# Two decoder blocks in one kernel: attention by pairs of heads, another order on ScalarE around a triangular inversion, and four PSUM banks in turn

## The chip, the cores and the metric

One Trainium2 chip, of which one core is used. The metric is device time in microseconds (us) of one execution of the whole program, from the first to the last instruction and what lies around them; lower is better. TensorE (PE) multiplies, VectorE (DVE), ScalarE (ACT) and GpSimd (POOL) work element by element, SyncE (SP) issues most DMAs. All five take their instructions in the order of their own queue.

## What is computed

`x` holds 512 tokens of 1024 features in float32. Two different blocks follow one another, each with two layers.

```python
# block 1, per layer
h = rms_norm(x, norm_mix[l])
(m_qk, m_v, m_o, m_i, m_f, r_x, r_g, a_q, a_k, a_v, a_qi, a_ki, a_w, gates) = split(h @ w_in[l])
y_a = mLSTM(silu(conv(m_qk)), m_v, m_i, m_f) * sigmoid(m_o)        # 4 heads of 128
y_b = gelu(r_g) * rg_lru(conv(r_x), ...)
y_c = dsa_attention(rope(a_q), rope(a_k), a_v, rope(a_qi), rope(a_ki), a_w)   # 8 heads of 64
x = x + (sum of sigmoid(gate_b) * (y_b' @ w_branch[b]) over the 3 branches) @ w_out[l]
x = x + (gelu(conv(ff_g)) * ff_u) @ ffn_down[l]
# dsa_attention, for each block of 128 queries:
score = sum_h w[q,h] * relu(q_idx[q,h] . k_idx[s]);  keep the 128 best visible keys of each query
p = softmax over those keys of q.k / 8;  out = p @ v
# block 2, per layer: RWKV-7 (chunks of 64 tokens), pooling branch, gates, gated FFN
S_t = S_{t-1} (diag(w_t) - kk_t^T (a_t*kk_t)) + v_t k_t^T ;  y_t = S_t r_t
y = (group_norm(y) * lnx_g + lnx_b + sum(r*k*r_k) * v) * g
```

## The kernel before

All activations lie transposed, 128 features by 512 tokens to a tile. A dense product of 128 output features (`lin_steps`, L490) takes 8 tiles of input; weights and inputs are each split into a rounded part H and a rest L of type float32r, and three matmuls (wh·hH, wh·hL, wl·hH) make up one step of the sum. 24 matmuls of 512 columns are one such product; each takes a PSUM bank by a tag and leaves it to a function of evacuation. Weights come by DMA from SP into three `raw` buffers; ACT casts them to `wh` (L432), DVE or POOL subtract to get `wl` (L433).

The program is written with generators that yield: `together` takes one step of each in turn, so dense products stand between the small steps of attention, mLSTM or RWKV ("fill"). A planner then orders each engine's queue by this written order, a cost model and due times; what it puts into a queue is fixed before the run.

**Block 1, `mix1`.** After the products for values, indexer and rope come `keys` (products aq and ak, with `dsa_mask` beside them), then `together(dsa(...), fill, beside())`, where `beside` holds the products qk, mv and mo. `dsa_mask(j)` makes for each of 8 indexer heads a product of two matmuls (L818 with all 128 rows, L819 with the 64 rows of one half), and finds the best 128 keys in 16 rounds on DVE (L831, L832). It runs for j = 1, 2, 3, with 128(j+1) keys. `dsa_attend(j)` goes head by head: one plain float32 matmul over 64 rows for the logits (L845), a softmax on DVE and ACT, up to four transposes (L861), and j+1 plain float32 matmuls with 64 output columns for the values (L868). The profile has two records for each plain float32 matmul. Then `mlstm` computes its gates (L893 to L917) and its heads; `rglru` and three `merge`s follow. PSUM's eight banks are shared as lin 3, pv 1, pb 2, at 2.

**Block 2, `mix2`.** `Rwkv.prep` and `prep_r` make decayed keys and queries for four pairs of heads (ksq L1550, rnb L1561, ar L1593 and L1603) beside the products 2k and 2r. `invert` multiplies them (am L1642), copies blocks into `room` and inverts 32 x 32 triangles by a serial chain on DVE (L1654 to L1668), beside a fill of 31 steps (`lent(fill, 31)`: products 2v, 2p, 2g1). `ready(0)` copies the inverse back (L1682, in turn on ACT, DVE and POOL), transposes it (L1685) and starts the chain of the chunks with L1689 (px). The evacuation of product 2v calls `bonus` (L1606 to L1624); that of 2p is the ACT copy `yb` (L1386), after which `pool` works on DVE (L1393 to L1398).

Of the kernel before, what the change touches and what calls it, by code (L numbers as in the profile page):

```python
# [9 lines left out]
F32 = mybir.dt.float32  # L10
# [8 lines left out]
KD = 8  # L19
# [291 lines left out]
def kernel(ctx: ExitStack, tc: tile.TileContext, aps: dict, out: bass.AP, taps=None, stop=None,  # L311
# [33 lines left out]
    def MX(name, tag="lin"):  # L345
        return cur[tag][0].tile([128, 512], F32, name=name, tag="p" + tag)
# [127 lines left out]
    def lin_steps(key, mts, hs, evac, first=0, last=0, tag="lin", fine=0):  # L474
# [19 lines left out]
        if first:  # L494
            ps = [MX("lnt", t) for t in {"at": ("at", "at", "lin", "lin"), "T2": ("T2",) * 3,
                                         "x": ("x", "x", "x", "lin")}[first_of("at", "T2", "x")][:first]]
# [13 lines left out]
        for m in range(first, mts - last):  # L510
            units = {g: u for g, u in units.items() if g >= m // gm}
            fetch(m, None)
            ps = MX("lnt", tag if isinstance(tag, str) else tag[m % len(tag)])
# [18 lines left out]
    def lin_tokens(key, l, hs, evac):  # L532
# [3 lines left out]
        ps = [MX("lnt", t) for t in ("at", "at", "lin", "lin")]  # L536
# [181 lines left out]
    def merge(*a):  # L718
        for _ in merge_steps(*a):
            pass  # L720

    def merge_steps(key_g, key_b, l, hs, ys, merged, tag, ytag, fine=0, done=None):
# [22 lines left out]
        sg, sb = lin_steps((key_g, l), 8, hs, evg, fine=fine), lin_steps((key_b, l), 8, yhl, evb, fine=fine)  # L745
# [91 lines left out]
    def dsa_attend(j, q, k, v, mk, yc):  # L837
        wd = 128 * (j + 1)
# [19 lines left out]
        def transposed(h):  # L858
            tp = MX("tp", "at")
# [11 lines left out]
        for h in range(8 + 4):  # L871
            if h < 8:
                softmax(h)
                yield
            if 0 <= h - 2 < 8:
                transposed(h - 2)
                yield
            if h >= 4:
                values(h - 4)
                yield  # L880
# [9 lines left out]
    def mlstm(smt, l, q, k, v, mo, ya):  # L890
# [3 lines left out]
        T1 = U("T1", "t")  # L894
        G.memset(T1, 0.0)
        af = U("af", "t")
# [3 lines left out]
        ls = U("ls", "t")  # L900
        V.tensor_scalar(ls[r], smt[rf], ifb[rf], 0.0, op0=ALU.add, op1=ALU.min)
        V.tensor_sub(ls[r], ls[r], af[r])
        ip = U("ip", "t")
        V.tensor_scalar(ip[r], smt[r], ifb[r], None, op0=ALU.add)
        g = U("g", "t")
        V.tensor_tensor_scan(g[r], C("ones")[r, 0:1].to_broadcast([4, S]), ls[r], 0.0, op0=ALU.mult, op1=ALU.add)
        m = U("m", "t")
        V.tensor_tensor_scan(m[r], ls[r], ip[r], 0.0, op0=ALU.add, op1=ALU.max)
        gm = U("gm", "t")
        V.tensor_sub(gm[r], g[r], m[r])  # L910
# [609 lines left out]
    class Rwkv:  # L1520
# [14 lines left out]
        def prep(self, p):  # L1535
# [22 lines left out]
            for _ in range(3):  # L1558
                yield
# [341 lines left out]
```

## Time and profile before

| | |
|---|---|
| median of 3 runs | 3645.12 us (3644.09 to 3647.41) |
| profiled execution, its own time | 3652.54 us |
| its span, first to last instruction | 3650.1 us |
| PE busy | 3537.1 us, 97% |
| DVE, ACT, POOL busy | 59%, 41%, 21% |
| mean granted clock of PE | 0.986 of full speed |

A matmul's duration in the profile holds the way through the array, and the next one starts before it ends; what a matmul takes of PE's time is the distance from its start to the next start. A form such as 64*128 gives the rows and columns of the array that a matmul uses.

### The profile page before, as it was taken

What the parts mean: (1) busy time and instruction counts of PE and PEld (TensorE: products, weight loads), DVE (VectorE), ACT (ScalarE), POOL (GpSimd) and SP (SyncE); (2) the same over time, 40 slices, a digit from 0 to 9 for tenths busy, and PEclk for the clock granted to TensorE, in tenths of its full rate; (3) what the DMA queues carried; (4) which work ended last, traced back from release to release, by engine and by line L of the source; (5) the groups of instructions that cost most, each with busy time, mean ns of one, the idle gap of its engine ahead of it and who ended that gap; (6) DMA issues with size and microseconds to landing.
All of it is one profiled execution on the core that took longest, in us unless ns stands there. A gap on an engine that the chain in (4) does not pass through costs nothing.

```text
span 3650.1 us, 48877 instructions
## 1 busy us (share of the span) xinstructions
PE 3537.1 (97%) x18160; PEld 2806.6 (77%) x18160; DVE 2160.7 (59%) x4586; ACT 1503.1 (41%) x2838; POOL 776.8 (21%) x637
## 2 busy tenths in 40 slices
PE   7999999999999999999999988999999889999998
PEld 6667788888886677888888766788888757788887
DVE  6864535666658546356767785564345884473445
ACT  4555533333335546233333544333223544342223
POOL 3523311000035233110000463320000652320000
PEclk9999999999999999999999989999999989999999
DMA  4212232455522123224545211222223211322222
GB/s 134 90 49 68 94 98 93 145 180 167 173 77 89 49 68 101 92 99 136 186 153 176 83 64 56 90 93 93 93 96 108 75 56 58 102 93 87 98 93 75
DMA packets 124894, 367.61 MB, mean 101 GB/s; under 512 B 14704, under 2 KB 19056, under 8 KB 124656
## 3 DMA queue, kind: packets, MB, share of 16 engines
q1 hardware_dynamic: 119264, 357.15, 29.7%
q10 hardware_dynamic: 5392, 7.35, 0.8%
q8 instruction: 142, 2.33, 0.3%
q14 instruction: 96, 0.79, 0.1%
HBM read 350.28 MB, written 7.34 MB: 98 GB/s over the span
## 4 chain that ended last, share of the span: by engine, by line
PE 87%; DVE 9%; ACT 2%; issue 1%; DMA 1%; POOL 0%; SPq 0%; DVEq 0%; ACTq 0%; POOLq 0%
PE lnt L490 77%; PE at L845 1%; PE pv L868 1%; DVE tm L1662 1%; PE lnt L548 1%; DVE sums L1665 1%; DVE bk L1590 1%; PE am L1642 1%; DVE wl L433 1%; DVE hn L634 1%; PE tp L861 1%; PE sp L941 0%; PE is L819 0%; ACT wh L432 0%; DVE hL L644 0%
## 5 line engine op out<-in xcount | busy, mean ns | idle before, releaser
L432 ACT CAST wh<-raw 128x512 fp32r<-128x512 f32 x1096 | 669.5, 619 | 1503.5 <-PE lnt L490 1423.3
L490 PE MATMUL lnt<-hH,wh 128*128 128x512 f32 (+1 forms) x3184 | 1264.4, 398 | 20.6 <-ACT yb L1386 18.7
L490 PE MATMUL lnt<-hL,wh 128*128 128x512 f32 (+1 forms) x3184 | 1227.7, 386 | 2.1 <-DVE hL L644 2.1
L490 PE MATMUL lnt<-hH,wl 128*128 128x512 f32 (+1 forms) x3184 | 1229.2, 386 | 0.0
L433 DVE TENSOR_TENSOR wl<-raw,wh 128x512 fp32r<-128x512 f32 x772 | 538.6, 706 | 649.8 <-ACT wh L432 646.9
L433 POOL TENSOR_TENSOR wl<-raw,wh 128x512 fp32r<-128x512 f32 x324 | 440.2, 1364 | 1482.2 <-ACT wh L432 1438.7
L490 PEld LDWEIGHTS lnt<-hH,wh 128*128 128x128 f32 x3184 | 603.0, 190 | 190.7 <-issue 44.0
L490 PEld LDWEIGHTS lnt<-hL,wh 128*128 128x128 f32 x3184 | 604.0, 190 | 130.3 <-issue 9.8
L490 PEld LDWEIGHTS lnt<-hH,wl 128*128 128x128 f32 x3184 | 603.2, 189 | 130.4 <-issue 2.7
L490 PE MATMUL lnt<-fH,wh 128*128 128x512 f32 (+1 forms) x864 | 313.9, 364 | 0.0
L490 PE MATMUL lnt<-fL,wh 128*128 128x512 f32 (+1 forms) x864 | 313.3, 363 | 0.1
L490 PE MATMUL lnt<-fH,wl 128*128 128x512 f32 (+1 forms) x864 | 312.8, 362 | 0.0
L490 PEld LDWEIGHTS lnt<-fL,wh 128*128 128x128 f32 x864 | 163.0, 189 | 28.5 <-DVE fL L408 0.5
L490 PEld LDWEIGHTS lnt<-fH,wh 128*128 128x128 f32 x864 | 163.0, 189 | 28.3
L490 PEld LDWEIGHTS lnt<-fH,wl 128*128 128x128 f32 x864 | 163.0, 189 | 27.7
L590 POOL TENSOR_TENSOR sums<-sums,sq 128x256 f32<-128x256 f32 (+1 forms) x61 | 54.3, 896 | 562.9 <-ACT sq L588 561.8
L1301 DVE SCALAR_TENSOR_TENSOR x<-lnt,mod,x 128x512 f32<-128x512 f32 (+1 forms) x136 | 88.9, 655 | 88.3 <-PE lnt L490 88.0
L696 DVE SCALAR_TENSOR_TENSOR cv<-lnt,vec,cv 128x511 f32<-128x511 f32 (+1 forms) x168 | 124.1, 745 | 14.7 <-ACT cv L694 13.2
L490 PE MATMUL lnt<-yH,wh 128*128 128x512 f32 x320 | 129.3, 404 | 0.0
L490 PE MATMUL lnt<-yH,wl 128*128 128x512 f32 x320 | 127.7, 399 | 0.0
L490 PE MATMUL lnt<-yL,wh 128*128 128x512 f32 x320 | 126.8, 396 | 0.0
L1282 DVE CUSTOM_DVE_ANT_0 adaw<-adaw,csilu 128x512 f32<-128x512 f32 x192 | 125.0, 686 | 1.3 <-DMA adaw<-in_ada_dram 1.1
(393 smaller groups left out, 4280.1 us busy)
## 6 DMA issues: line engine op xcount, KB each, us to landing
raw<-in_wst_dram SPq DMA_DIRECT2D x548, 512.0 KB, 3.3
adaw<-in_ada_dram SPq DMA_DIRECT2D x192, 256.0 KB, 3.4
sw<-rq ACTq DMA_DIRECT2D x96, 64.0 KB, 2.0
xd<-x SPq DMA_DIRECT2D x16, 256.0 KB, 3.1
x<-xd SPq DMA_DIRECT2D x16, 256.0 KB, 3.5
x<-in_xT_dram SPq DMA_DIRECT2D x8, 256.0 KB, 6.0
out_dram<-x SPq DMA_DIRECT2D x8, 256.0 KB, 2.2
csilu<-in_c_dram SPq DMA_DIRECT2D x4, 256.0 KB, 5.4
```

The lines of the kernel that those rows point to most:

```text
L432: A.copy(h[:, :q], raw[:, sl])
L433: sub(l[:, :q], raw[:, sl], h[:, :q].bitcast(F32), op=ALU.subtract)
L490: mm = T.matmul(ps[:, sl], w_, h_[:, sl], start=(k == 0 and i == 0), stop=(k == kt - 1 and i == 2))
L548: T.matmul(ps[t], h_[:, o], w_, start=(k == 0 and i == 0), stop=(k == KD - 1 and i == 2))
L590: G.tensor_tensor(acc[:, sl], acc[:, sl], sq[:, sl], op=ALU.add)
L634: V.scalar_tensor_tensor(h, x[k][:, sl], g[:, k:k + 1], sums[0][:, sl], op0=ALU.mult, op1=ALU.mult)
L696: V.scalar_tensor_tensor(y[:, d:], ps[:, :S - d], taps_w[nt - 1 - d], y[:, d:], op0=ALU.mult, op1=ALU.add)
L845: T.matmul(ps[:, :wd], q[p][r, j * 128:j * 128 + 128], k[p][r, :wd], start=True, stop=True)
L861: T.transpose(tp[:, i * 128:i * 128 + 128], lgs[h][:, i * 128:i * 128 + 128], ident)
L868: T.matmul(pv[r, p * 128:p * 128 + 128], v[i][:, h * 64:h * 64 + 64], pts[h][:, i * 128:i * 128 + 128], start=(i == 0), stop=(i == j))
L1282: V.tensor_tensor_reduce(out=w, in0=w, in1=t, scale=1.0, scalar=0.0, op0=ALU.mult, op1=ALU.add, accum_out=sm[:, i:i + 1])
L1301: return V.scalar_tensor_tensor(x[m][:, sl], ps[:, sl], md[:, o + m:o + m + 1], x[m][:, sl], op0=ALU.mult, op1=ALU.add)
```

## The change

**Block 1.** q and k leave rope as H and L parts (one ACT copy and one DVE subtraction per tile, 8 tiles a layer). `logits(p)` makes the logits of two heads with six float32r matmuls, three terms, the two heads in turn, each into its own bank of a two-bank tile. `values(p)` runs the two heads of a pair in turn. L819 now takes all 128 rows. The mLSTM gates (`mgates`) run beside the attention of the last block of queries; six steps of dense work come ahead of the attention. The convolved qk tiles are kept in `x`, which is fetched again before the merges (from the input in layer 0, from a copy in DRAM in layer 1). Banks are now lin 2, pv 1, pb 3, and one tile of two banks, a2; the products of keys and of the merges take banks of several tags in turn.

**Block 2.** The copy rnb waits until ksq of the next pair is in ACT's queue. `bonus` is cut in two: `values` stays in the evacuation of 2v, the rest comes 14 matmul groups later, as one DVE multiplication from PSUM; the bias is added in `gate`. The first four of the fill's 31 steps come ahead of `invert`. The copies of `ready(0)` are all on DVE.

```diff
-    def MX(name, tag="lin"):
-        return cur[tag][0].tile([128, 512], F32, name=name, tag="p" + tag)
+    def MX(name, tag="lin", banks=1):
+        return cur[tag][0].tile([128, banks * 512], F32, name=name, tag="p" + tag)
...
             A.copy(q, ps)
-            lst.append(U(nm, tag))
-            rope(q, 128, lst[m], ps)
+            o = U("ro", "t")
+            rope(q, 128, o, ps)
+            lst.append(split(o, nm, tag))
...
-            qe, high = qi[p][e], slice(64 * e, 64 * e + 64)
-            T.matmul(ps[:, :wd], qe[:, j * 128:j * 128 + 128], kid[0][:, :wd], start=True, stop=False)
-            T.matmul(ps[:, :wd], qe[high, j * 128:j * 128 + 128], kid[1][high, :wd], start=False, stop=True)
+            qe = qi[p][e]
+            for i, t in enumerate(kid):
+                T.matmul(ps[:, :wd], qe[:, j * 128:j * 128 + 128], t[:, :wd], start=(i == 0), stop=(i == 1))
...
-        def softmax(h):
-            p, r = h // 2, slice(64 * (h % 2), 64 * (h % 2) + 64)
-            ps = MX("at", "at")
-            T.matmul(ps[:, :wd], q[p][r, j * 128:j * 128 + 128], k[p][r, :wd], start=True, stop=True)
+        def logits(p):
+            (qh, ql), (kh, kl) = q[p], k[p]
+            at = MX("at", "a2", 2)
+            pss = [at[:, e * 512:e * 512 + 512] for e in range(2)]
+            for i, (q_, k_) in enumerate(((qh, kh), (ql, kh), (qh, kl))):
+                for e, ps in enumerate(pss):
+                    r = slice(64 * e, 64 * e + 64)
+                    T.matmul(ps[:, :wd], q_[r, j * 128:j * 128 + 128], k_[r, :wd], start=(i == 0), stop=(i == 2))
+            return pss
+
+        def softmax(h, ps):
...
-            tp = MX("tp", "at")
+            tp = MX("tp", "pb")
...
-        def values(h):
-            p, r = h // 2, slice(64 * (h % 2), 64 * (h % 2) + 64)
+        def values(p):
             for i in range(j + 1):
-                T.matmul(pv[r, p * 128:p * 128 + 128], v[i][:, h * 64:h * 64 + 64], pts[h][:, i * 128:i * 128 + 128],
-                         start=(i == 0), stop=(i == j))
...
+                for h in (2 * p, 2 * p + 1):
+                    r = slice(64 * (h % 2), 64 * (h % 2) + 64)
+                    T.matmul(pv[r, p * 128:p * 128 + 128], v[i][:, h * 64:h * 64 + 64],
+                             pts[h][:, i * 128:i * 128 + 128], start=(i == 0), stop=(i == j))
...
-                yield
-                yield
+                for _ in range(3):
+                    yield
                 yt = MX("yt", "pb")
...
+        if l:
+            for k in range(KD):
+                nc.sync.dma_start(xd[k], x[k])
...
+            for _ in range(4):
+                yield
             for j in (1, 2, 3):
...
+            banks = ("lin", "pv", "lin", "a2")
...
-            s = U("qk", "fm")
+            s = x[m]
...
+        def gates():
+            while 3 not in masks:
+                yield
+            yield from mgates(smt, l, gated)
+
+        dense = beside()
+        for _ in lent(dense, 6):
+            pass
+        together(dsa(q, k, v, masks, yc), fill, gates(), dense)
...
-        together(mlstm(smt, l, qk[:4], qk[4:], mv, mo, ya), lent(fill, 42))
+        together(mlstm(*gated, qk[:4], qk[4:], mv, mo, ya), lent(fill, 42))
...
+        for i in range(KD // 2):
+            if l:
+                for k in (2 * i, 2 * i + 1):
+                    nc.sync.dma_start(x[k], xd[k])
+            else:
+                nc.sync.dma_start(x2[i], pair(aps["xT"], i, ALL))
+        merge("g0", "br0", l, hs, [(y, mnh[:, i:i + 1]) for i, y in enumerate(ya)], merged, "fd", "fd", bank=("lin", "pb"))
...
-            rw.bonus(m)
+            rw.values(m)
+            later.append([14, lambda: rw.bonus(m)])
...
-        together(rw.invert(), lent(fill, 31))
+        for _ in lent(fill, 4):
+            pass
+        together(rw.invert(), lent(fill, 27))
...
-                V.tensor_mul(y[p], y[p], gp)
+                V.scalar_tensor_tensor(y[p], y[p], VC("lb", l)[:, p:p + 1], gp, op0=ALU.add, op1=ALU.mult)
...
-            A.activation(sq, kf[p], ACTF.Square, scale=kcol)
+            self.sq.append(A.activation(sq, kf[p], ACTF.Square, scale=kcol).ins)
...
+            while len(self.sq) < min(p + 2, 4):
+                yield
             rb = U("rnb", "f", (128, 8, 64))
-            A.copy(rb, rn.unsqueeze(2).to_broadcast([128, 8, 64]))
+            with tc.issue_after(self.sq[-1]):
+                A.copy(rb, rn.unsqueeze(2).to_broadcast([128, 8, 64]))
...
-            G.tensor_tensor(y[p], y[p], vf[p], op=ALU.mult)
-            A.activation(y[p], y[p], ACTF.Identity, bias=VC("lb", l)[:, p:p + 1])
+
+        def bonus(self, p):
+
+            bp = MX("bp")
+            T.matmul(bp, C("bones"), self.rr[p], start=True, stop=True)
+            V.tensor_mul(self.y[p], self.vf[p], bp)
...
-                    cp_ = (A.copy, V.tensor_copy, G.tensor_copy)[(2 * n + e) % 3]
+                    cp_ = (A.copy, V.tensor_copy, G.tensor_copy)[(2 * n + e) % 3] if Q else V.tensor_copy
...
-                for _ in range(3):
+                for _ in range(5):
                     yield
                 tail()
...
-                with phase(dict(fd=20, sc=3, rl=2, t=8, fm=16), dict(lin=3, pv=1, pb=2, at=2)):
+                with phase(dict(fd=20, sc=3, rl=2, t=8, fm=16), dict(lin=2, pv=1, pb=3, a2=1)):
```

## Rows read from the trace of the kernel before

**Rows 1.** The page, busy time of each engine over the span.

```profile
PE 3537.1 (97%) x18160; PEld 2806.6 (77%) x18160; DVE 2160.7 (59%) x4586; ACT 1503.1 (41%) x2838; POOL 776.8 (21%) x637
```

**Rows 2.** Windows: start:end, length, busy us of five engines, granted clock, DMA.

```profile
95.00:235.00 140.00, 140.00 (x581) 89.78 (x581) 115.47 (x308) 74.39 (x181) 60.88 (x48) 1.00 0.24 74
235.00:300.00 65.00, 64.36 (x302) 45.54 (x302) 14.04 (x38) 36.03 (x70) 18.55 (x18) 1.00 0.17 57
2090.00:2150.00 60.00, 47.31 (x195) 35.65 (x195) 52.48 (x77) 27.13 (x47) 43.92 (x40) 0.80 0.15 49
2150.00:2226.00 76.00, 61.31 (x327) 47.52 (x325) 64.66 (x166) 36.99 (x75) 38.02 (x32) 0.89 0.21 69
```

**Rows 3.** Groups by line and shape, PE, both layers: records, busy us, mean ns.

```profile
L868 PE MATMUL pv<-pt,v 128*64 128x128 f32 x320 | 49.9, 284 | 0.0
L845 PE MATMUL at<-k,q 64*128 64x512 f32 x32 | 18.0, 641 | 0.0
L845 PE MATMUL at<-k,q 64*128 64x128 f32 x32 | 7.8, 322 | 0.0
```

**Rows 4.** Timeline of PE, two dense matmuls in a row: start us, duration us.

```profile
200.91 0.39 PE L490 MATMUL lnt<-hH,wh 128*128 128x512 f32 x1
201.14 0.39 PE L490 MATMUL lnt<-hL,wh 128*128 128x512 f32 x1
```

**Rows 5.** Timeline of PE, logits of one head between three dense matmuls.

```profile
196.62 0.50 PE L490 MATMUL lnt<-hH,wh 128*128 128x512 f32 x1
...
198.36 0.50 PE L490 MATMUL lnt<-hH,wh 128*128 128x512 f32 x1
```

**Rows 6.** Timeline of PE, values of two heads, three dense matmuls between.

```profile
266.16 1.09 PE L868 MATMUL pv<-pt,v 128*64 128x128 f32 x8
...
268.06 1.09 PE L868 MATMUL pv<-pt,v 128*64 128x128 f32 x8
```

**Rows 7.** Timeline of PE, one indexer head (L818, L819), then one dense matmul.

```profile
78.94 0.28 PE L818 MATMUL is<-kH,qe 128*128 128x256 f32 x1
...
79.80 0.40 PE L490 MATMUL lnt<-hL,wh 128*128 128x512 f32 x1
```

**Rows 8.** Windows of two lines whose products alternate between halves: PE, PEld (records).

```profile
2154.20:2155.05 0.85, 0.84 (x14) 0.84 (x16) 1.00 0.00 0
...
2253.29:2254.25 0.96, 0.96 (x32) 0.96 (x32) 1.00 0.00 0
```

**Rows 9.** Costliest groups of the page: a DVE subtraction of 512 columns.

```profile
L433 DVE TENSOR_TENSOR wl<-raw,wh 128x512 fp32r<-128x512 f32 x772 | 538.6, 706 | 649.8 <-ACT wh L432 646.9
```

**Rows 10.** Line L845 in 57:300 us, who waited for it (us, times).

```profile
  DVE lg L848: 20.3, 14
```

**Rows 11.** DMA issues of the page: count, KB each, us from issue to landing.

```profile
raw<-in_wst_dram SPq DMA_DIRECT2D x548, 512.0 KB, 3.3
```

**Rows 12.** Waits of PE: total us, times, longest.

```profile
PE lnt L490 <- ACT yb L1386: 18.7, 2, 14.5
PE n L1554 <- ACT ksq L1550: 12.8, 4, 5.3
PE am L1642 <- DVE ar L1603: 11.7, 2, 6.0
...
PE lo L1348 <- ACT x L1611: 7.4, 1, 7.4
...
PE ytt L1816 <- DVE yn L1811: 5.3, 4, 1.7
```

**Rows 13.** Timeline around the end of the inversion, layer 0 of block 2.

```profile
2201.93 0.82 ACT L1682 COPY ah<-room 32x128 f32<-32x128 f32 x2 [16.11 <-DVE room L1668]
...
2201.93 5.70 DVE L1682 COPY ah<-room 32x128 f32<-32x128 f32 x12
...
2222.01 1.29 DVE L1685 STREAM_TRANSPOSE tn<-ah 32x128 f32<-32x128 f32 x4
...
2225.56 0.69 PE L1689 MATMUL px<-tn,ah 32*32 32x32 f32 x32
```

More of the change, by code (lines that the diff above doesn't have):

```diff
@@ L494, in lin_steps @@
         if first:
-            ps = [MX("lnt", t) for t in {"at": ("at", "at", "lin", "lin"), "T2": ("T2",) * 3,
-                                         "x": ("x", "x", "x", "lin")}[first_of("at", "T2", "x")][:first]]
+            ps = [MX("lnt", t) for t in {"T2": ("T2",) * 3,
+                                         "x": ("x", "x", "x", "lin")}[first_of("T2", "x")][:first]]
             for m in range(first):
@@ L535, in lin_tokens @@
         units = []
-        ps = [MX("lnt", t) for t in ("at", "at", "lin", "lin")]
+        ps = [MX("lnt", t) for t in ("pb", "pb", "lin", "lin")]
         for c in range(4):
@@ L716, in lent, with merge, merge_steps @@
             yield
-    def merge(*a):
-        for _ in merge_steps(*a):
+    def merge(*a, **k):
+        for _ in merge_steps(*a, **k):
             pass
-    def merge_steps(key_g, key_b, l, hs, ys, merged, tag, ytag, fine=0, done=None):
+    def merge_steps(key_g, key_b, l, hs, ys, merged, tag, ytag, fine=0, done=None, bank="lin"):
         yhl = [split(y, "y", ytag, sc) for y, sc in ys]
@@ L888, in dsa, with mgates @@
             yield from dsa_attend(j, q, k, v, masks[j], yc)
-    def mlstm(smt, l, q, k, v, mo, ya):
+    def mgates(smt, l, out):
         ifb = VC("ifb", l)
@@ L893, in mlstm @@
         rf = slice(96, 100)
-        T1 = U("T1", "t")
+        T1 = sums[0]
         G.memset(T1, 0.0)
-        af = U("af", "t")
+        V.tensor_copy(pick[r], ident[r, 64:68])
+        af = U("af", "rl")
         A.activation(af[r], smt[rf], ACTF.Abs, bias=ifb[rf], scale=1.0)
         A.activation(af[r], af[r], ACTF.Exp, scale=-1.0)
+        yield
         A.activation(af[r], af[r], ACTF.Ln, bias=1.0)
-        ls = U("ls", "t")
+        ls = U("ls", "rl")
         V.tensor_scalar(ls[r], smt[rf], ifb[rf], 0.0, op0=ALU.add, op1=ALU.min)
+        yield
+        V.tensor_scalar(T1[r], smt[r], ifb[r], None, op0=ALU.add)
+        yield
         V.tensor_sub(ls[r], ls[r], af[r])
-        ip = U("ip", "t")
-        V.tensor_scalar(ip[r], smt[r], ifb[r], None, op0=ALU.add)
-        g = U("g", "t")
+        yield
+        g = af
         V.tensor_tensor_scan(g[r], C("ones")[r, 0:1].to_broadcast([4, S]), ls[r], 0.0, op0=ALU.mult, op1=ALU.add)
[L907 to L910, printed above, removed]
-        Gt = [U("Gt" + n, "t", dt=F32R) for n in "HL"]
-        A.copy(Gt[0][r], gm[r])
-        V.tensor_sub(Gt[1][r], gm[r], Gt[0][r].bitcast(F32))
-        pick = sp.tile([128, 4], F32R, name="pick", tag="pick", bufs=1)
-        V.tensor_copy(pick[r], ident[r, 64:68])
-        V.tensor_sub(T1[r], ip[r], g[r])
+        yield
+        yield
+        m = sums[1]
+        V.tensor_tensor_scan(m[r], ls[r], T1[r], 0.0, op0=ALU.add, op1=ALU.max)
+        yield
+        yield
+        V.tensor_sub(ls[r], g[r], m[r])
+        V.tensor_sub(T1[r], T1[r], g[r])
         A.activation(T1[rf], m[r], ACTF.Exp, scale=-1.0)
         yield
+        Gt = [U("GtH", "t", dt=F32R), U("GtL", "fd", dt=F32R)]
+        A.copy(Gt[0][r], ls[r])
+        V.tensor_sub(Gt[1][r], ls[r], Gt[0][r].bitcast(F32))
+        out.extend([T1, Gt])
+        yield
+    pick = sp.tile([128, 4], F32R, name="pick", tag="pick", bufs=1)
+    def mlstm(T1, Gt, q, k, v, mo, ya):
+        r = slice(64, 68)
         tp = MX("tc", "pb")
@@ L974, in give @@
                                     op1=ALU.mult)
-                yield
-                yield
+                for _ in range(3):
+                    yield
                 yt = MX("yt", "pb")
@@ L1139, in chosen @@
             n = 0
+            for _ in range(4):
+                yield
             for j in (1, 2, 3):
@@ L1148, in keys @@
         def keys():
-            yield from lin_steps(("aq", l), 4, hs, rope_ev(q, "q", "fd"), fine=1)
-            yield from lin_steps(("ak", l), 4, hs, rope_ev(k, "k", "fd"), fine=1)
-        lin_fm(("qi", l), 4, hs, ev_qi)
+            banks = ("lin", "pv", "lin", "a2")
+            yield from lin_steps(("aq", l), 4, hs, rope_ev(q, "q", "fm"), tag=banks, fine=1)
+            yield from lin_steps(("ak", l), 4, hs, rope_ev(k, "k", "fd"), tag=banks, fine=1)
+        lin_fm(("qi", l), 4, hs, ev_qi, tag=("lin", "lin", "pv"))
         heads(3)
@@ L1184, in beside @@
                 yield from g_
-        together(dsa(q, k, v, masks, yc), fill, beside())
+        gated = []
+        def gates():
+            while 3 not in masks:
+                yield
+            yield from mgates(smt, l, gated)
[3 more added lines that the diff above has]
+        together(dsa(q, k, v, masks, yc), fill, gates(), dense)
         del q, k, v, qi, kid
@@ L1202, in beside @@
             yield from lin_steps(("rg", l), 4, hs, ev_rg, fine=2)
-            yield from merge_steps("g2", "br2", l, hs, [(y, 1.0) for y in yc], merged, "fd", "fd", 2)
+            yield from merge_steps("g2", "br2", l, hs, [(y, 1.0) for y in yc], merged, "fd", "fd", 2, None,
+                                   ("lin", "pv", "lin", "a2"))
         merged = [None] * 8
         fill = beside()
-        together(mlstm(smt, l, qk[:4], qk[4:], mv, mo, ya), lent(fill, 42))
+        together(mlstm(*gated, qk[:4], qk[4:], mv, mo, ya), lent(fill, 42))
         tap(f"ya{l}", ya)
```

50 lines of the change are left out of this document (25 added, 25 removed).

## The prediction

> **What bounds the kernel now.** I read the page first. PE is busy for 3537.1 of 3650.1 us [rows 1], so what the change is worth is the PE time that it takes away, plus the PE waits that it ends. [...]
>
> **Attention, the price of a column.** A dense matmul of 512 columns starts 0.23 us after the one before [rows 4], 0.45 ns a column. The logits' records last 641 ns at 512 columns and 322 at 128 [rows 3]: 0.83 ns a column and record, and a product has two records. Three float32r terms would so cost 1.35 ns a column against 1.66, a small gain; the larger question is whether the two heads of a pair run at once. No row shows the new logits, so I take the nearest. Line L1788 writes alternate halves of 64 output columns: 32 records of 64 columns, 0.053 us each, are done within 0.96 us [rows 8], where one after another they would take 1.70. Line L1642 alternates halves of 64 rows: 14 records of 128 columns, 0.106 us each or 1.48 together, lie in 0.85 us [rows 8]. Both kinds of halves run two at a time, and that is what I take; the other bound is that they don't.
>
> **Attention, the price of an interruption.** From 196.62 to 198.36 there are three dense matmuls (0.69 us) and one head's logits of 2 x 384 columns (0.64 us); 0.41 us is left [rows 5]. From one head's values to the next's, 1.90 us, three dense matmuls (0.69) and eight records of 128 columns (0.85) leave 0.36 [rows 6]. One indexer head with one dense matmul takes 0.86 us; its two matmuls of 256 columns and the dense one are 0.46 us of columns: 0.40 us is left [rows 7]. So each stretch of products in another shape costs about 0.4 us beside its columns.
>
> **Attention, the sum for a layer.** Blocks of 128 to 512 keys and 8 heads make 10,240 logit columns.
> Logits now: 10,240 x 1.66 ns = 17.0 us, and 32 stretches x 0.41 = 13.1, together 30.1. After: 5,120 x 1.35 ns = 6.9, and 16 x 0.41 = 6.6, together 13.5. Gain 16.6 (unpaired: 13.8 + 6.6 = 20.4, gain 9.7).
> Values now: 160 records x 0.106 = 17.0, and 32 x 0.36 = 11.5, together 28.5. After: 8.5 + 5.8 = 14.3. Gain 14.2 (unpaired: 5.7).
> Indexer: L819 over all rows keeps the shape of the dense products. 24 heads x 0.40 = 9.6 us.
> Sum 40.4 us a layer, 80.8 in both; unpaired 25.0 and 50.0.
>
> [...]
>
> **What of it arrives.** Two things beside PE must keep up. DVE has 115.5 us to do in 95 to 235, and gets eight subtractions of 0.71 us [rows 9] for q and k: 121.2. In that stretch PE loses blocks 0 to 2 (24 of the 32 stretches and 6/10 of the columns: logits 11.0, values 9.4) and 16 indexer heads (6.4), 26.8 of its 140 us, so 113.2 stay: DVE is short by 8.0 us. Against this, DVE itself waits 20.3 us for these logits [rows 10], and dense products can be ordered ahead. After 235 DVE has 14 of 65 us to do [rows 2], so the gates, which are moved there, are covered: two activation tables more in ACT's queue, ahead of later softmaxes, with ACT at 36 of 65 [rows 2]. I take 5 us a layer off, from 0 to 8 and, if the planner orders it badly, 20: **35 us a layer, 70 in both**.
>
> ACT's eight more casts lie in a stage where it is busy 74 of 140 us [rows 2]: nothing; without that cover they are about as long as DVE's eight. The banks: dense products beside attention fall from three to two, and a bank is held while ACT and three passes of DVE read it; the next product takes 24 x 0.23 = 5.5 us and more, which covers that. If the cover is gone, it is the rival on the other side, below. The x copies are 2 MB a layer; SP's queue holds the weight loads behind them. A copy back waits for the last reader of qk, which by the written order is done before `rglru`. Four loads as long as one of weights, 3.3 us [rows 11], hold the queue for 13 us, while three buffers of weights are 3 x 24 x 0.23 = 17 us of PE work. I count nothing; without this cover, 13 us a layer. The third yield in the mLSTM and the fewer waits there: 1 us, not counted.
>
> **Block 2.** Five PE waits stand there [rows 12]: on yb 18.7 us (two), on ksq 12.8 (four), on ar 11.7 (two), on the low-rank product L1348 7.4, on ytt 5.3 (four). What is late next decides, so I follow the path. ACT stands 16.11 us for the end of the inversion because copies L1682 are at the head of its queue, and yb is behind them; PE waits for yb [rows 12, 13]. With the copies of the first chunks on DVE, and `bonus` out of ACT's queue, yb comes in time; the copies of later chunks may still stand ahead of it, which I can't see. Four steps of fill ahead of `invert`, 4 x 6 x 0.23 = 5.5 us, cover the wait for ar, but only move work: PE is limited next by px, which needs the transposes L1685. Now: the inversion ends at 2201.9, px starts at 2225.6 [rows 13]. Afterwards: eight copies at 5.70/12 = 0.48 us, 3.8, and transposes, 1.3, give px at 2207.0 if DVE does nothing else first: 18 us gained. If the pooling on DVE still stands between, as in the 14.4 us from 2207.6 to 2222.0 now, px comes at 2221.4: 4 us gained. I take 11 a layer, midway, since both can be seen coming; in the second layer the waits on ar, L1348 and yb are as much (5.7 + 7.4 + 4.2). The low clock (0.80 and 0.89 in the windows) comes back with it in part and is inside these numbers. The ksq wait: DVE is busy 52.5 of 60 us there, and rnb(p) now has to wait for the next pair's ksq, so I count 0, between a gain of its 6.4 us and a loss of one more such wait, 3.2, a layer. ytt: two more yields end half of 5.3: 3. **Block 2: 2 x 11 + 3 = 25 us.**
>
> **Sum.** 3652.5 - 70 - 25 = 3557.5 for the profiled execution. The median of the runs is 7.4 us lower, and I predict that: **3550 us**.
>
> **The rivals.**
> (a) *The halves don't pair.* For it: the new logits are float32r and long, and no row has two such at once in this order. Against it: both lines of [rows 8]. Block 1 gains 50 - 10 = 40: 3652.5 - 40 - 25 - 7.4 = 3580.
> (b) *DVE becomes the bound of the attention.* For it: 121 us of work in a stretch that would shrink to 113, in an order fixed before the run. Against it: it waits on PE itself [rows 10]. Each layer gains 20: 3645 - 40 - 25 = 3580.
> (c) *The edits of block 2 don't do what they say:* ACT still stands before yb because a planner puts the copies of later chunks first, and px waits for DVE anyway. For it: the wait for px is on DVE's serial chain. 3645 - 70 - 3 = 3572, or 3575.
> (d) *Slower: two banks for the dense products beside attention and mLSTM.* The 8 products qk and 4 products rx of a layer hold their bank until DVE has made three passes, on a DVE that is busy over 80%. The price is the wait per product times 24; it decides from 95/24 = 4 us per product, and 6 us would give 3645 - 95 + 144 = 3694. Against it: DVE's passes follow each other within one product's time now.
>
> **How the numbers follow.** The forecast, 3550, has 0.60, with its own range 3515 to 3570: at the low end all 81 us, 2 x 18 and 3 us, and some clock (10); above it (c) begins. (a) has 0.12, (b) 0.12, (c) 0.10, (d) 0.04, and 0.02 is left. The range for 8 in 10 goes from 3512 to 3594: (a), (b) and (c) are in it, with 4 us of block 2 in place of 11 in each layer. Below 0.2% (7 us) this kernel's runs can't be told from no change. All cases but (d) are faster: 0.94; same 0.02; slower 0.04.
>
> **What would show it.** In the profile after: logits as 64*128 records of 0.45 ns a column whose starts come in twos; L868 the same with 128*64; L819 as 128*128; the length of each layer's attention, 75 to 300 now, down by about 35 us; no PE wait there over 1 us. In block 2: the ACT wait of 16 us before L1682 gone, px about 11 us earlier after the first am, no PE wait on L1348. The prediction is wrong if dense matmuls in the attention wait for banks or DVE, or if a new PE wait stands where yb's stood.

## The result, and the profile after

The changed kernel takes 3600.28 us (median of 4 runs, 3597.30 to 3603.08) against 3645.01 us of the kernel before on the same chip: ratio 0.9876, 95% interval 0.9859 to 0.9893. It is 44.7 us faster. The forecast was 3550 (3512 to 3594): the sign was right, the gain less than half of the 95 us expected. The profiled execution has 3597.30 us and a span of 3595.5. It lies 3 us below its kernel's median, and the profiled execution of the kernel before (3652.54) 7 us above its own, so the two traces differ by 55 us, not 45; most of the excess lies in block 2.

The page, busy time of each engine (the answer to [rows 1]): PE has 63 us less to do and is still the busiest, at 97%.

```profile
PE 3474.0 (97%) x18224; PEld 2792.3 (78%) x18224; DVE 2150.7 (60%) x4620; ACT 1503.0 (42%) x2836; POOL 761.2 (21%) x625
```

Windows of the kernel after; the first two are those of [rows 2], the last two end at px as in [rows 2], which now stands 45 us earlier.

```profile
95.00:235.00 140.00, 131.54 (x646) 95.96 (x645) 119.70 (x314) 84.16 (x198) 63.33 (x50) 0.99 0.24 76
235.00:300.00 65.00, 63.15 (x342) 48.12 (x340) 18.33 (x64) 36.17 (x77) 18.63 (x18) 1.00 0.21 70
2050.00:2110.00 60.00, 50.56 (x217) 38.87 (x217) 54.69 (x86) 27.95 (x47) 46.44 (x44) 0.86 0.19 63
2110.00:2181.00 71.00, 59.73 (x304) 44.92 (x302) 61.88 (x176) 32.57 (x67) 30.63 (x25) 0.95 0.20 70
```

In the attention, where PE had no idle time at all, 8.5 of 140 us are idle now. Around the inversion the two windows have 20.7 us idle in place of 27.4, at a granted clock of 0.86 and 0.95 for 0.80 and 0.89.

Where the time came from is seen in windows of whole stages: for each layer of block 1 from its first product to the first gate product of `rglru`, then for each layer of block 2 from the product "out" ahead of it to the last product of `gate`. First the kernel before:

```profile
19.50:382.50 363.00, 357.96 (x1562) 254.49 (x1563) 233.77 (x604) 189.64 (x413) 136.04 (x109) 1.00 0.23 72
1029.90:1391.10 361.20, 357.06 (x1564) 254.47 (x1563) 219.69 (x575) 184.70 (x405) 138.15 (x112) 1.00 0.23 73
1586.30:2360.20 773.90, 737.04 (x4384) 598.75 (x4383) 532.12 (x1205) 320.75 (x596) 162.47 (x142) 0.97 0.35 117
2413.70:3161.40 747.70, 712.46 (x4236) 574.11 (x4235) 426.88 (x890) 289.06 (x542) 161.68 (x135) 0.97 0.26 84
```

The same stages of the kernel after:

```profile
20.20:365.70 345.50, 331.81 (x1594) 251.50 (x1595) 236.14 (x612) 196.43 (x424) 136.63 (x109) 1.00 0.26 82
1016.10:1355.70 339.60, 328.76 (x1595) 249.89 (x1596) 221.54 (x576) 188.82 (x411) 136.18 (x108) 0.99 0.27 86
1550.60:2316.40 765.80, 736.37 (x4385) 597.88 (x4384) 529.43 (x1214) 314.99 (x585) 154.67 (x136) 0.98 0.36 118
2369.80:3107.70 737.90, 704.27 (x4236) 568.15 (x4235) 422.69 (x899) 283.23 (x531) 152.40 (x129) 0.98 0.26 86
```

Block 1 gained 17.5 and 21.6 us (724.2 to 685.1), block 2 8.1 and 9.8; the stretch between the two layers of block 1 lost 3.0. Other executions of the same block 2 put its gains lower: 775.6 and 742.6 us in e7, which has it as before, and 769.9 and 737.8 in e15, which is the kernel after once more. In block 1 PE's busy time fell by 54.5 us, but its idle time (length less busy) rose from 9.2 to 24.5.

Two pairs of heads in PE's timeline after. A whole block of 512 keys:

```profile
239.60 0.50 PE L852 MATMUL at<-kH,qH 64*128 64x512 f32 x2 [0.62 <-DVE mrow L858]
239.93 0.40 PE L852 MATMUL at<-kH,qL 64*128 64x512 f32 x2
240.16 0.39 PE L852 MATMUL at<-kL,qH 64*128 64x512 f32 x2
240.49 0.50 PE L490 MATMUL lnt<-hH,wl 128*128 128x512 f32 x1
```

And a block that the issue order cuts in two:

```profile
248.14 0.50 PE L852 MATMUL at<-kH,qH 64*128 64x512 f32 x1
248.57 0.43 PE L879 MATMUL pv<-pt,v 128*64 128x128 f32 x2
248.94 0.50 PE L852 MATMUL at<-kH,qH 64*128 64x512 f32 x1
...
249.83 0.51 PE L490 MATMUL lnt<-hH,wl 128*128 128x512 f32 x1
```

The whole block takes 0.89 us for six products of 0.23: two run at a time. The cut one holds PE for 1.69 us with 0.37 of values in it, so 0.43 more than the whole one: the first head's product stands alone in the issue order, ahead of two products of values. The issue order of PE has the 32 logits blocks of both layers in 50 stretches and the 32 values blocks in 58, 108 in place of 64.

PE's waits after (total us, times, longest), beside [rows 12]:

```profile
PE Rn L1623 <- ACT rnb L1618: 16.0, 4, 4.9
...
PE lnt L490 <- DVE x L1681: 7.7, 1, 7.7
...
PE at L852 <- DVE nmrow L861: 6.0, 3, 4.0
PE vt L1779 <- DVE x L1673: 5.1, 1, 5.1
...
PE ytt L1873 <- DVE yn L1868: 3.5, 4, 0.9
PE n L1608 <- ACT ksq L1604: 3.2, 2, 1.6
PE lnt L549 <- DVE x L1093: 2.9, 1, 2.9
...
PE p L1454 <- ACT yb L1438: 2.4, 1, 2.4
```

The waits on yb (18.7 to 1.1 and 2.4; 1.1 and 5.9 in the repeat e15), ksq (12.8 to 3.2), ar (11.7) and the low-rank product (7.4) are gone or small. In their place stand 16.0 on rnb and, on DVE, 7.7 and 5.1 on bonus's multiplication (L1681; the 5.1 ahead of the product bp), 5.1 on a pass of `values` (L1673) and 2.9 on x between the layers. In the attention PE now waits for the softmax (nmrow, once for 4.0 us).

### The profile page after: what moved, and what is told of

It reads as the page before. It is cut to its first block, busy times and chain, and to the rows that moved or that the text cites. A ratio compares the mean times of both kernels' runs of the same rounds, so it can differ in the third digit from the quotient of the medians.

```text
span 3595.5 us, 48989 instructions
## 1 busy us (share of the span) xinstructions
PE 3474.0 (97%) x18224; PEld 2792.3 (78%) x18224; DVE 2150.7 (60%) x4620; ACT 1503.0 (42%) x2836; POOL 761.2 (21%) x625
## 4 chain that ended last, share of the span: by engine, by line
PE 82%; DVE 12%; ACT 3%; issue 1%; POOL 1%; DMA 1%; ACTq 0%; SPq 0%; DVEq 0%; POOLq 0%
PE lnt L490 74%; PE lnt L549 1%; DVE sc L834 1%; DVE m L833 1%; DVE tm L1719 1%; DVE sums L1722 1%; DVE hn L635 1%; PE am L1699 1%; PE sp L968 1%; ACT wh L432 1%; PE pv L879 1%; DVE bk L1647 1%; ACT lg L863 0%; DVE hL L645 0%; DVE ah L1739 0%
## 5 line engine op out<-in xcount | busy, mean ns | idle before, releaser
L490 PE MATMUL lnt<-hH,wh 128*128 128x512 f32 (+1 forms) x3184 | 1257.4, 396 | 11.9 <-DVE x L1681 7.7
L490 PEld LDWEIGHTS lnt<-hH,wh 128*128 128x128 f32 x3184 | 603.7, 190 | 158.5 <-issue 14.6
L697 DVE SCALAR_TENSOR_TENSOR cv<-lnt,vec,cv 128x511 f32<-128x511 f32 (+1 forms) x168 | 124.0, 744 | 16.5 <-ACT cv L695 14.9
```

The lines of the kernel that those rows point to most:

```text
L490: mm = T.matmul(ps[:, sl], w_, h_[:, sl], start=(k == 0 and i == 0), stop=(k == kt - 1 and i == 2))
L697: V.scalar_tensor_tensor(y[:, d:], ps[:, :S - d], taps_w[nt - 1 - d], y[:, d:], op0=ALU.mult, op1=ALU.add)
```

## The experiments

All were run like the kernel after, against the kernel before (3644 to 3646 us), 4 runs each and 11 for e5 and e7. "Block 1" is the length of the two windows above in the profiled execution (724.2 before, 685.1 after). Single executions of one kernel differ by up to 13 us (e2), so medians of four that are a few us apart say little. The changed kernel run again (e15) had 686.5 in block 1, 1.4 above the first time, and 769.9 in place of 765.8 in the first layer of block 2, where PE was busy 1.9 us longer and idle 2.3 longer, at a granted clock of 0.98 both times.

| run | median us | ratio, 95% interval | block 1 |
|---|---|---|---|
| e1 block 1 alone | 3609.76 | 0.9902 (0.9886 to 0.9919) | 684.9 |
| e2 heads singly | 3605.86 | 0.9889 (0.9874 to 0.9905) | 693.9 |
| e3 blocks whole | 3583.79 | 0.9838 (0.9823 to 0.9853) | 680.8 |
| e4 rnb order undone | 3607.91 | 0.9895 (0.9881 to 0.9910) | 686.7 |
| e5 light before | 3649.38 | 1.0013 (1.0004 to 1.0021) | 726.9 |
| e6 light after | 3595.62 | 0.9866 (0.9852 to 0.9879) | 683.1 |
| e7 indexer alone | 3642.53 | 0.9995 (0.9986 to 1.0004) | 717.9 |
| e8 inversion undone | 3605.81 | 0.9897 (0.9883 to 0.9910) | 685.2 |
| e9 casts behind | 3593.73 | 0.9864 (0.9848 to 0.9881) | 686.1 |
| e10 bonus's bank | 3601.76 | 0.9880 (0.9865 to 0.9894) | 687.6 |
| e11 e3 + e9 + e10 | 3585.59 | 0.9840 (0.9825 to 0.9855) | 676.7 |
| e12 light, whole | 3588.05 | 0.9847 (0.9833 to 0.9862) | 677.4 |
| e13 banks moved | 3594.43 | 0.9867 (0.9851 to 0.9884) | 684.2 |
| e14 e3 + e9 + e13 | 3588.74 | 0.9847 (0.9832 to 0.9862) | 678.0 |
| e15 after again | 3600.59 | 0.9878 (0.9863 to 0.9892) | 686.5 |

**e1, which block the gain is from.**

```diff
-            rw.values(m)
-            later.append([14, lambda: rw.bonus(m)])
+            rw.bonus(m)
...
-            with tc.issue_after(self.sq[-1]):
-                A.copy(rb, ...)
+            A.copy(rb, ...)
```

> The changed kernel with its edits in block 2 taken back (bonus, inversion, order of rnb, gates). It divides the gain of 45 us. By the landmarks of the two traces, block 1 gives about 36 us of the 55 that the profiled executions differ by, block 2 about 18: then this kernel takes 3609 to 3617 us. By the sum of the prediction block 1 is worth 70 us: 3575. If block 2 had eaten a full gain of block 1, this kernel would be the faster one, below 3595.

Block 1 is worth 36 us of the 45, where the forecast had 70; block 2's edits add 9.5 for 25. The two intervals overlap a little, but every execution of e1 is slower than every one of the kernel after.

**e2, the order within a pair.**

```diff
-            for i, (q_, k_) in enumerate(...):
-                for e, ps in enumerate(pss):
+            for e, ps in enumerate(pss):
+                for i, (q_, k_) in enumerate(...):
```

> The changed kernel, but the two heads of a pair one after the other instead of product by product in turn, for the logits (L852) and the values (L879); nothing else. If the halves run two at a time, as the trace after shows for some pairs, the order is worth the columns of one half: 6.9 us of logits and 8.5 us of values a layer, 31 us in all, less about 3 us for stretches that this order has fewer of (the issue order has 100 in place of 108): 3628. Rival (a) of the prediction, no pairing: 3600, no difference.

The time is 5.6 us above the kernel after, with overlapping intervals; in the trace block 1 is 8.8 us longer. That is near what rival (a) expects, but the timeline shows another reason. PE's rows of this kernel, logits of one pair and values of another:

```profile
240.48 0.51 PE L852 MATMUL at<-kH,qH 64*128 64x512 f32 x2 [0.68 <-DVE mrow L858]
240.82 0.40 PE L852 MATMUL at<-kH,qL 64*128 64x512 f32 x2
241.04 0.40 PE L852 MATMUL at<-kL,qH 64*128 64x512 f32 x2
241.38 0.50 PE L490 MATMUL lnt<-hH,wl 128*128 128x512 f32 x1
...
257.25 1.58 PE L879 MATMUL pv<-pt,v 128*64 128x128 f32 x16 [0.43 <-ACT pt L873]
258.76 0.44 PE L871 MATMUL tp<-cst,lg 128*128 128x128 f32 x2
```

Three products of one head and then three of the other still start in twos and take the same 0.90 us: the edit did not unpair the logits. The 16 values products took 1.51 us, where 14 in turn take 1.01 in the kernel after (255.82 to 256.83). So rival (a) is false by the timeline, and this run measures only what turn by turn adds for the values. (One head's 8 values records take 1.02 us in the kernel before, 266.16 to 267.18, as long as 14 in turn take in the kernel after.)

**e3, blocks kept whole.** The six logits products of a pair, and the values products of a pair, follow each other in a fixed order that begins with the head that comes free last.

```diff
-                for e, ps in enumerate(pss):
-                    T.matmul(ps[:, :wd], q_[r, ...], k_[r, :wd], ...)
+                for e in (1, 0):
+                    ps, r = pss[e], slice(64 * e, 64 * e + 64)
+                    with tc.issue_after(ins) if ins else ExitStack():
+                        ins = T.matmul(ps[:, :wd], q_[r, ...], k_[r, :wd], ...).ins
```

> The changed kernel, but the six products of a pair's logits and the products of a pair's values are tied into one order, beginning with the head that comes free last. In the issue order of PE the logits and values then stand in 74 stretches in place of 108 (32 blocks each, both layers). Theory S, that the gain of the attention fell short because the blocks were cut into more stretches than one a pair, each at about 0.4 us: 34 x 0.4 = 14 us less, 3586. Theory D, that PE now waits for DVE's softmax and savings on PE come back as idle time: no gain, 3598 to 3608, with longer PE waits before L852.

16.5 us below the kernel after in the median; the intervals don't overlap. Its block 1 in windows:

```profile
20.10:363.40 343.30, 327.79 (x1594) 250.21 (x1595) 236.21 (x612) 195.88 (x424) 136.86 (x109) 0.99 0.27 83
1013.60:1351.10 337.50, 323.87 (x1595) 247.82 (x1596) 220.86 (x576) 188.26 (x411) 136.92 (x108) 0.99 0.28 87
```

In this execution (3593.4, the slowest of the four; the others lie at 3583 to 3584) block 1 is only 4.3 us shorter. PE is busy 8.9 us less than in the kernel after, though 5.1 us more of its busy time are lost to half clock, and idle 4.6 more. So the trace shows that theory S holds for PE's work (14.0 us) and that two thirds of it came back as idle time and low clock, as theory D expects, though it leaves open what PE waits for. Where the other three executions have 10 us more is not shown, as they left no trace.

**e4 and e8, the two halves of block 2's edits.** e4 undoes the order of rnb behind the next ksq; e8 undoes all the others of block 2 and keeps that order.

```diff
-            with tc.issue_after(self.sq[-1]):
-                A.copy(rb, ...)
+            A.copy(rb, ...)
```

> The changed kernel without the new order of ACT's queue before the inversion (rnb of a pair behind the next pair's ksq). The prediction counted it as nothing. The trace after has 16 us of PE waits on rnb (four) in place of 12.8 on ksq and 11.7 on ar. If the new wait only takes the place of the old ones: 3598 to 3603, with the waits on ksq back. If the order is a loss of its own: 3588 to 3594. If it gained: 3606 to 3612.

```diff
-        for _ in lent(fill, 4):
-            pass
-        together(rw.invert(), lent(fill, 27))
+        together(rw.invert(), lent(fill, 31))
...
-                    cp_ = (...)[(2 * n + e) % 3] if Q else V.tensor_copy
+                    cp_ = (...)[(2 * n + e) % 3]
```

> The changed kernel with the edits around the inversion taken back (bonus through ACT and at once, no fill ahead of invert, the first copies on three engines, gates as before), but with the new order of ksq and rnb in ACT's queue kept. Block 2's edits together are worth 9.5 us (run e1), the order of rnb 7.6 (run e4). If the prediction's step holds (px earlier, 2 x 11 us) this kernel takes 3618 to 3623; if the order of rnb is most of block 2's gain, 3600 to 3604.

The order of rnb is worth 7.6 us, the edits around the inversion 5.5, both together 9.5 (e1). e8 lies between the two ranges that were expected of it. The sizes are good to some 3 us, and still the term that was counted as nothing is as large as the one that was counted as 22.

**e5, e6, DVE's load taken away.** Both kernels, the one before and the one after, leave out 12 of the 16 rounds of the selection.

```diff
-        for r in range(TOPK // 8):
+        for r in range(TOPK // 32):
```

> The kernel before with 4 of the 16 rounds of the top-k selection on DVE (12 rounds for each of three blocks left out, 43 us of DVE work a layer by the profile); it is the yardstick for the next run. PE was never idle in this stage before, so it should gain nothing: 3640 to 3648 us.

> The changed kernel with 4 of the 16 rounds of the top-k selection, beside the run with the same cut in the kernel before. Theory D, that DVE (rival (b) of the prediction) takes back the gain of the attention: freed of 43 us a layer it lets the gain grow from 45 to the 75 or more of the prediction's sum, 3570 or less. Theory S, more stretches than counted: the gain stays 40 to 52 us, since PE's products and their stretches are the same; 3593 to 3603.

Between these two the gain is 53.8 us instead of 44.7; 4.2 of the 9 come from e5 itself, which is slower than the kernel before, against what was expected, and no run explains that. The rounds left out are 43 us a layer when their records are added up, but DVE's busy time in block 1's windows fell by less, 28 to 31 us a layer. DVE's load takes some of the gain, not the missing 34 us: theory D is wrong as a matter of load.

**e7, the indexer alone.**

```diff
-            T.matmul(ps[:, :wd], qe[high, j * 128:j * 128 + 128], kid[1][high, :wd], start=False, stop=True)
+            for i, t in enumerate(kid):
+                T.matmul(ps[:, :wd], qe[:, j * 128:j * 128 + 128], t[:, :wd], start=(i == 0), stop=(i == 1))
```

> The kernel before with one part of the change alone: the indexer's second product over all 128 rows (L819 in the form of the dense products). The prediction's term is 24 x 0.40 = 9.6 us a layer: 3626. By PE's steps in the two traces (15.0 us of L818 and L819 a layer before, 11.1 after) it is worth 4 a layer: 3637.

2.7 us, and the interval reaches no change. Its block 1:

```profile
18.90:380.10 361.20, 352.02 (x1562) 255.85 (x1563) 237.85 (x604) 189.42 (x413) 136.84 (x109) 1.00 0.22 73
1027.50:1384.20 356.70, 348.35 (x1564) 253.76 (x1563) 223.59 (x575) 184.45 (x405) 139.00 (x112) 1.00 0.23 74
```

PE has 14.6 us less to do, 7.3 a layer for the 9.6 forecast. But its idle time, 9.2 before, is 17.5: 8.3 of the 14.6 came back as waits at once; in layer 0 the new ones are on the indexer's own ACT step (rl, 2.1) and on the softmax (mrow, 1.8). Block 1 is 6.3 us shorter in this trace, more than the median shows.

**e9, e10, e13: one wait at a time.** e9 puts the split of a rotated q or k behind the next product's copy in ACT's queue; e10 gives bonus's product a bank of the chain; e13 lists the banks in another order.

```diff
-            lst.append(split(o, nm, tag))
+            if wait:
+                with tc.issue_after(i.ins):
+                    lst.append(split(wait.pop(), nm, tag))
...
-            bp = MX("bp")
+            bp = MX("bp", "ch")
...
-dict(lin=2, pv=1, pb=3, a2=1)
+dict(lin=2, pv=1, a2=1, pb=3)
```

> The changed kernel, but the new split of a rotated q or k into its two halves (L407 and L408 of rope_ev) stands behind the next product's copy in ACT's queue, where in the changed kernel it stands among the DMA issues of the next rotation and waits for POOL: 12.3 + 5.0 us of ACT waits on POOL's ro in the first layer, with 8.6 us of DVE waits behind them, and PE gaps of 2.1 and 3.95 us at 125 and 140, the second with 3.4 us at half clock after it; the second layer has the like (5.9 us of gaps, 3.4 us at half clock). Theory W, that these casts, which the prediction counted as nothing, cost the waits: both layers' gaps and low clock go, 12 to 15 us, 3585 to 3588. If the attention's start is bound by something else: 3597 to 3603.

ACT's waits on ro fell from 17.3 to 12.0 us in layer 0 and DVE's on kH from 8.6 to 2.6, but block 1 is no shorter (686.1): the PE gap moved from 140 to 133, where the first logits wait for DVE's multiplication of the last k (ro L797), which reads a bank that they need. Where the 6.5 us of its median come from is not settled; the intervals overlap, and in the profiled execution block 2's second layer is 3.0 shorter.

> The changed kernel, but the product of bonus (bp) writes a bank of the chain's tag in place of one of the two that the dense products take in turn. After, dense products of block 2 wait 7.7 us in the first layer and 1.1 in the second for DVE's multiplication of bp, transposes vt 5.1 for it, and two of the low-clock stretches (6.8 and 10.2 us, half of them lost) follow. If the bank is the cause of those waits, 10 to 18 us come off: 3582 to 3590. If DVE's queue is late whatever the bank: vt waits on it anyway, 3597 to 3603.

No gain. ACT's timeline of this kernel, layer 0 of block 2, and PE's total of the wait that came:

```profile
2168.20 3.73 ACT L1739 COPY ah<-room 32x128 f32<-32x128 f32 x9 [6.37 <-DVE room L1725]
...
2173.01 0.58 ACT L1438 COPY yb<-lnt 128x512 f32<-128x512 f32 x1
...
PE p L1454 <- ACT yb L1438: 20.5, 2, 10.3
```

PE is released 10.3 us late in each layer by a copy of yb that frees a bank, and this copy stands in ACT's queue behind nine copies that wait for the end of the inversion. It is the wait of rival (c), which is 2.4 us in the changed kernel (5.9 in e15) and came back when the other one went.

> The changed kernel with the banks of the attention stage listed in another order (pb last), so that the first products of layer 1 do not write the banks that ffn1 frees last. After, PE's first product of that layer waits 2.9 us for DVE's add (x L1093), where before it had no such wait, and the stretch from the first layer's recurrence to this product is 3.0 us longer (650.4 for 647.4). If the place of the banks is the cause, that stretch is 647.5 again and the time about 3 us lower, 3597; if not, 650.

The stretch is 647.3 us again: the 3.0 us between the layers came from the place of the banks in PSUM. The median is 5.9 us lower; what goes beyond 3.0 is within the scatter.

**e11, e12, e14: together.**

> Blocks whole (run e3), casts behind (run e9) and the bonus's bank (run e10) in one kernel. If the three losses stand at different places they add up: e3 alone measured 3584, less the gains of e9 and e10 against 3600, so 3555 to 3570 where both theories hold, which is near the prediction's 3550. If the whole blocks and the casts remove the same wait: 3575 to 3584.

> Whole blocks (e3), casts behind (e9) and the moved banks (e13), without e10's bank of the bonus, which gained nothing. If block 1 keeps e11's 8.4 us and the banks give 3: 3580, below e3 and e11 at 3584 to 3586; if the gains are swallowed by later waits, 3584 to 3590.

Neither beats e3 in the time, though their block 1 is 4.1 and 2.8 us shorter than e3's: the repairs don't add up.

> Blocks whole (run e3) and 4 of the 16 rounds of the top-k selection (runs e5 and e6) at once: nearly one stretch a block (68 for 64 blocks, both layers) and DVE freed of 43 us a layer, beside e5 at 3649. If cut blocks and waits for DVE's chains are what the prediction's sum of 80.8 us for block 1 lost, both layers from their first product to the recurrence (726.9 us in e5) shrink by 65 us or more, and the time is 3565 to 3577. If the prices of the sum were wrong themselves, the stage shrinks by 50 us or less, as in e3 (46 with scatter), 3583 to 3592.

Block 1 of the light kernel before (e5), then of e12:

```profile
20.10:384.50 364.40, 359.42 (x1562) 254.45 (x1563) 204.40 (x496) 189.58 (x413) 137.17 (x109) 1.00 0.22 72
1031.90:1394.40 362.50, 358.18 (x1565) 254.09 (x1564) 191.32 (x467) 184.56 (x405) 139.26 (x112) 1.00 0.23 73
```

```profile
19.30:359.70 340.40, 326.52 (x1594) 248.00 (x1595) 208.78 (x504) 195.03 (x424) 137.64 (x109) 0.99 0.26 83
1010.00:1347.00 337.00, 324.28 (x1594) 247.22 (x1595) 191.59 (x468) 187.81 (x410) 137.16 (x108) 0.98 0.28 87
```

The stage shrinks by 49.5 us, not 65. By the fork of the expectation that would mean wrong prices, but a third case shows: PE is busy 66.8 us less, 73.6 with the low clock taken out, near the 80.8 of the sum, and idle 17.3 more. With DVE at 61% and 57% of the stage's length, PE's waits in layer 0's attention are short ones on steps of the chain, the longest 1.7 us:

```profile
PE is L821 <- ACT rl L823: 4.4, 6, 1.4
PE at L854 <- DVE mrow L860: 2.7, 3, 1.2
```

> The changed kernel once more, for the scatter of the stages between profiled executions: 3597 to 3603 as a time, block 1's two layers within 1 us of 685.1, block 2's two halves within some 5 us of 765.8 and 737.9, by the stretches at half clock.

## Why the prediction missed

The balance of block 1, both layers, from the windows; "half clock" is half of the time that the granted clock stood at 0.50 of full speed there (from the clock's own records; the windows round it), and PE's work is its busy time less that. The half is an estimate: in 140.95:144.36 of the kernel after, at a clock of 0.50, dense matmuls start 0.43 us apart (141.34, 141.76, 142.19), against 0.23 in [rows 4], at 1.00.

| | PE's work saved | more idle | more half clock | shorter by |
|---|---|---|---|---|
| the sum of the prediction | 80.8 | 10 in all | | 70 |
| after | 56.2 | 15.4 | 1.7 | 39.1 |
| e3 blocks whole | 70.2 | 20.0 | 6.8 | 43.4 |
| e12 beside e5 | 73.6 | 17.3 | 6.8 | 49.5 |
| e7 indexer alone | 14.6 | 8.3 | 0.0 | 6.3 |

**The prices were right.** A whole block of 512 keys takes 0.89 us and 0.1 more on the dense product on either side, 1.09, where the prediction had 0.69 + 0.41 = 1.10. The halves pair; rival (a) is false. With the stretches that each kernel has beyond 64 at 0.4 us, and with 4.6 for the indexer, the work saved comes to 78.4 (after), 78.8 (e3) and 79.8 (e12, 68 stretches) of the 80.8. In a block of 128 keys the six products, with their loads of weights, all start within 0.27 us, the loads of the two halves together and the next two 0.11 us later (at 153.18, 153.29 and 153.40), where the 128 columns of a product are 0.06 us by the price of 0.45 ns. PE's rows of a block of 128 keys:

```profile
153.19 0.33 PE L852 MATMUL at<-kH,qH 64*128 64x128 f32 x2
153.35 0.28 PE L852 MATMUL at<-kH,qL 64*128 64x128 f32 x2
153.46 0.27 PE L852 MATMUL at<-kL,qH 64*128 64x128 f32 x2
```

Of the 31.7 us that block 1 fell short of its 70.8 in the trace, 24.6 are PE's work and 7.1 waits and clock.

**First failed step: "16 stretches x 0.41" (logits) and the like for values.** It took one stretch a pair for given. The order had 108 for 64; e3, which ties a block's products from the operand that is ready last, has 74, so a likely reason is that the planner lets a block's first product go when its own bank or operand is ready. 44 x 0.4 = 17.6 us of the 24.6 that PE's work fell short; e3 shows it: with 34 stretches fewer PE's work saved is 14.0 higher. The indexer's term was 4.6 too high in both layers (14.6 for 19.2).

**Second failed step: "I take 5 us a layer off".** PE's idle time and half clock took 17.1 us in both layers, not 10, and in e12, where DVE is light and the blocks are whole, 24.1 of 73.6. The prediction looked for the limit in DVE's load (113 us for 121); e6 and e12 show that taking some 30 us a layer of that load away gives 4.7 us more of block 1 with the blocks cut and 6.1 with them whole. What returns are waits of 1 to 4 us on the chain product, softmax or relu, next product, in an order fixed beforehand. The likely reading is that before, PE's slow products covered them, and each product that is made faster uncovers some: e7 makes only the indexer's products cheaper, and 8.3 of its 14.6 us return so. The prediction's own sign, no PE wait there over 1 us, was not met (nmrow 4.0). Rival (b)'s gain (20 a layer) was near what block 1 did, by another cause than the one it named.

**What was counted as nothing.** The x copies: no wait names them. The two banks: dense products wait 1.2 us for DVE's passes (cv); rival (d) did not occur. That two of the stage's banks are those which `ffn1` frees last was not seen; it cost 3.0 us (e13). The casts stand in ACT's queue among the next rotation's DMA issues and wait for POOL, 17.3 us in layer 0; e9 shows that this costs block 1 nothing as long as the keys' chain is late anyway.

**Block 2: 25 forecast, 9.5 measured.** The term that failed is "2 x 11 (px earlier)", less in its size than in taking px's lead as time saved. ACT's, DVE's and PE's queues at the end of the inversion, layer 0 after, beside [rows 13]:

```profile
2162.89 1.25 DVE L1725 STREAM_TRANSPOSE room<-sums 128x1024 f32<-128x1024 f32 x1
2164.17 4.24 DVE L1739 COPY ah<-room 32x128 f32<-32x128 f32 x8
2166.23 3.85 ACT L1739 COPY ah<-room 32x128 f32<-32x128 f32 x9
...
2171.60 3.96 DVE L1739 COPY ah<-room 32x128 f32<-32x128 f32 x7
...
2180.20 1.29 DVE L1742 STREAM_TRANSPOSE tn<-ah 32x128 f32<-32x128 f32 x4
2180.64 1.53 PE L1746 MATMUL px<-tn,ah 32*32 32x32 f32 x32 [1.70 <-DVE tn L1742]
```

DVE makes 17 copies, the eight counted and nine of later chunks, and pooling still stands between them and the transposes. From the end of the inversion to px it is 16.5 us for 23.7, and in the second layer 15.5 for 24.5: 16 us gained in both, for 22. ACT no longer stands before yb, as predicted, but px still waits for DVE, so rival (c) is half true. From the first am to px, the sign that the prediction names, the two layers are even 18.7 and 14.5 us shorter (13.1 and 11.9 in the repeat). But the stretches ahead of the first am, from block 1's last `rglru` and from the first layer's px, grew by 9.2 and 10.9 us (7.8 and 10.7). The four steps of fill stand there now, 5.5 us each time by the prediction's own price, which it did not charge; the rest is not explained, and no run undoes these steps alone. The ksq order, counted as 0 between a gain of 6.4 and a loss of 3.2 a layer, is worth 7.6 us in both (e4), although four waits on rnb took the place of those on ksq: PE's waits on ksq, ar and rnb are 19.2 us with it and 21.0 without, so where the rest comes from is open. ytt: 5.3 to 3.5, 2 us for 3.

The sum then: block 1 36 for 70, block 2 9.5 for 25, together 45 for 95. What remains open is which of the chain's steps would have to shorten for e3's idle 20 us to come back. Of three tries at single waits, e9 and e10 moved them elsewhere, and e13 ended the wait between the layers, but not those of the attention.

## What to carry over

When PE never waits and its products get cheaper, price what comes back: the idle time that the slow products had covered. Here 30 to 57% of PE's savings in block 1 were lost so, to idle time and low clock, also with DVE at 60% (e12), and removing one of the waits mostly moved it. And a price per stretch holds only if the order keeps the stretch together: count the stretches in the issue order, and tie the products of a block to each other, beginning with the operand that comes last (e3: 14 us of PE's work for a few lines, 16.5 us in the median). And when work is moved out of a wait, price what it costs where it goes.

## What the hardware showed beside that

- Products of the two row halves run side by side even if the program writes three of one half ahead of three of the other: 0.90 us for six of 512 columns in e2 (240.48 to 241.38), as when they alternate. The first terms of both heads start at 240.48 there and the second terms at 240.82, so the product written fourth starts 0.34 us ahead of the one written second; whether the planner or PE put it there, no run shows. Products of the two column halves, eight after eight, overlap only in part: 1.51 us for 16 (e2), 1.01 for 14 in turn (kernel after).
- A gap was followed by low clock. After the gap of 3.95 us that ends at 140.23 in the kernel after, PE's granted clock is 0.51 for 3.4 us (140.90:144.30) while it works without a pause, which costs 1.7 us more by the estimate above; in the kernel before this stage of layer 0 had clock 1.00 throughout. In e12, where PE's longest wait in the attention of layer 0 is 1.7 us, the clock is 0.50 for 6.8 us from 144.60, counted as 3.4. That a gap brings the low clock about, no run shows. PE's row behind the first gap, then the windows of low clock of the kernel after and of e12:

```profile
140.23 0.33 PE L852 MATMUL at<-kH,qH 64*128 64x128 f32 x2 [3.95 <-DVE nmrow L861]
140.90:144.30 3.40, 3.40 (x10) 2.92 (x10) 1.58 (x8) 1.71 (x5) 3.32 (x3) 0.51 0.00 0
144.60:151.40 6.80, 5.97 (x19) 4.39 (x18) 5.38 (x24) 3.80 (x8) 3.82 (x3) 0.50 0.26 92
```
